# Layer 1's left-over modulation parts move from the recurrence to the mixers, and the mixers' PSUM banks are cut anew

## The chip, the cores and the metric

The kernel runs on one core of a Trainium2 chip. The metric is the time of one execution in microseconds of device time. Before the change three runs took 2719.62, 2722.55 and 2728.21 us, so the median is 2722.55. One execution was also profiled.

## The reference: what is computed

The reference is a two-layer backbone on 512 latent and 256 context tokens, 1024 channels wide, all in float32. Each layer has three token mixers beside each other (a bidirectional RWKV-7 recurrence, a latent attention, a Fourier mixing), merged through sigmoid gates, and then a gated feed-forward part with a convolution:

```
mod_lat = silu(c) @ w_ada[l] + b_ada[l]            # six vectors of 1024: shift, scale, gate, twice
h       = rms(x) * g_norm1 * (1 + sc1) + sh1
a, b, f, gate = split(h @ w_in)
m  = sig(gA)*(rwkv(a) @ w_a) + sig(gB)*(attention(b) @ w_b) + sig(gC)*(fourier(f) @ w_c)
x  = x + gt1 * (m @ w_out)
x  = x + gt2 * conv_ffn(rms(x) * g_norm2 * (1 + sc2) + sh2)
```

The last layer needs outputs for the latent tokens alone. The change is about when layer 1's modulation vectors (the first line) are computed. The first four of the 24 half-vectors are computed at the start, the other twenty in the background of the two layers.

## The kernel before

A float32 product of the large projections is made of three products of split operands (high by high, high by low, low by high; H and L in the names). The program is written in Python; a scheduler then sets the order in which each engine's instructions stand, so the order on TensorE (PE), VectorE (DVE), ScalarE (ACT), GpSimd (POOL) and SyncE (SP) is fixed before the program runs. Every engine works through its own list in order; SyncE's list issues most DMAs.

A layer goes through these stages: the projections of the recurrence (rwkv_project), the recurrence itself (rwkv_scan, twelve steps, each of a chain of small products in the PSUM tags f, i0, i1 and st), the mixers (fourier, rwkv_out, mla), and then the branches, w_out and the feed-forward part. PSUM has eight banks, and CUTS says how each stage divides them into tags; a tag with two buffers can be filled by one product while the product before it is still read.

Beside the recurrence the class Background issues work from a list. Its items are gate parts (L688, tag w: 24 products of 128x512 in layer 1, then ScalarE writes the tile gt and stores it) and modulation parts (ada_part). A modulation part loads 2 MB of w_ada in four loads of 512 KB into the buffers wr (three buffers, which gate weights and later the mixers' weights use too), makes eight products with them (L258), copies the row with ScalarE (L261), transposes it with four products (L265), and adds it up on VectorE (L268). In the recurrence the modulation parts run aside, in a tag of their own (a), with each load issued one ahead; layer 1 has eight of them (ADAS[1]). A gate part gives way to a step of a modulation part at its end, and with MID also once in its middle (L691). After each block of the recurrence's products, after() lets the background run for a fixed amount. When the recurrence has been written, drain() issues what is left: before the change all gate parts and, in layer 1, all modulation parts. What is left of them after a drain is made into items by mix(); those run in the mixers wherever fill() stands, in tag w, without a load ahead. In layer 0 two parts do.

The buffers hH and hL hold the layer's normalized input, which the gate parts read. They are given back (hst.close()) once no item needs them, and the mixers' tiles, gT among them, take their place. In layer 1 the mixers begin with kr, the rotary part of the keys (raw is loaded from m_dram, L460, and transposed by L464); then the key and query projections (L394, 72 products of 128x384 and 72 of 128x288), whose heads are transposed by L452; fourier (L639 to L660, tag r) stores its result by L669; rwkv_out loads the recurrence's outputs y (L1226, L1227), adds them (L1230), and takes three tiles of columns through tag r: L1233 (means), L801 (sums of squares), VectorE's reciprocal root and ScalarE's rex (L806), L813 (back to rows), read by L1238. Then comes the attention: scores by L567, transposes by L584, values by L595, again in tag r; four buffers pt hold the transposed probabilities.

Of the kernel before, what the change touches and what calls it, by code (L numbers as in the profile page):

```python
# [47 lines left out]
for _n, _w in CCOLS:  # L48
# [15 lines left out]
TAGF, TAGO = ("r", "r"), ("s", "r")  # L64
ROF = True
MFILL, AFILL = 2.5, 0.3
FIRST = ((12, 2.0), (8, 3.0))
MORE = False
XB, UB = 2, 2
MID = (True, True)  # L70
FILL = (1.0, 0.8)
PRE = (12.0, 24.0)
CUTS = dict(
    dense=(("mm", 2), ("s", 3), ("w", 1)),
    scan=(("f", 2), ("i0", 1), ("i1", 1), ("st", 2), ("w", 1), ("a", 1)),
    mixers0=(("mm", 2), ("s", 2), ("r", 1), ("w", 1)),
    mixers1=(("mm", 2), ("s", 2), ("r", 2)),
)
SCHED = dict(schedule_with_timeline_sim=True)

# [2 lines left out]
def hybrid_backbone_kernel(ctx: ExitStack, tc: tile.TileContext, A, out, dbg=None):  # L83
# [11 lines left out]
    def psum_phase(l, name):  # L95

        if banks:
            banks.pop("es").close()
            banks.clear()
        banks["es"] = ExitStack()  # L100
        for tag, bufs in CUTS[name]:
            banks[tag] = banks["es"].enter_context(tc.tile_pool(name=f"ps_{name}{l}_{tag}", bufs=bufs, space=bass.MemoryType.PSUM, reuse_waits="tile"))
# [175 lines left out]
    def near(es, l, name, bufs=1):  # L278
        return pool_on(es, name, l % 2, bufs)

    def far(es, l, name, bufs=1):
        return pool_on(es, name, 1 - l % 2, bufs)

    class Norm:
# [75 lines left out]
        def after_gain(self, parts, ks):  # L360
            for a, b in parts:
                s = 0 if a < LAT else 1
                for k in ks:
# [3 lines left out]
                    self.low(k, a, b)  # L367

    def mla(l, last, others, load_y, fill):
        q_tiles = range(4) if last else range(6)  # L370
        with ExitStack() as e1, ExitStack() as e2:
# [109 lines left out]
            def kv_rows(cH, cL, yc, WH, WL):  # L481
                hs = work.tile([128, 6, 6], F32, name="hs")
                for t in range(6):
                    ps = psmm()
                    proj(ps, t, cH, cL, WH, WL, 2, 0, 384, 0)
                    proj(ps, t, cH, cL, WH, WL, 2, 384, 768, 512)
                    jk = work.tile([128, 576], F32, tag="f", name="jk", bufs=2)[:, 0:384]
                    S.activation(out=jk, in_=ps[:, 0:384], func=AF.Square, scale=yc[:, t:t + 1])
                    V.tensor_reduce(out=hs[:, t], in_=jk.rearrange("p (h d) -> p h d", d=64), op=ALU.add, axis=AX.X)
                    S.activation(out=kn[:, t], in_=ps[:, 0:384], func=AF.Copy, scale=yc[:, t:t + 1])  # L490
                    S.activation(out=Vn[:, t], in_=ps[:, 512:896], func=AF.Copy, scale=yc[:, t:t + 1])
                    fill()
                V.tensor_tensor(out=hs, in0=hs, in1=ks.to_broadcast([128, 6, 6]), op=ALU.add)
                return hs.rearrange("p t h -> p (t h)")

            def q_rows(cH, cL, yc, WH, WL):
                qn = work.tile([128, nqn], F32, tag="qn" if FRONT[l] else "kn", name="qn").rearrange("p (t h d) -> p t h d", t=nq, d=QK)
                hs = work.tile([128, 6, 6], F32, name="hq")[:, 0:nq]
                for t in q_tiles:
                    ps = psmm()  # L500
                    proj(ps, t, cH, cL, WH, WL, 3, 0, 288, 0)
                    proj(ps, t, cH, cL, WH, WL, 3, 288, 576, 512)
                    jq = work.tile([128, 576], F32, tag="f", name="jq", bufs=2)
                    pv = ps.rearrange("p (a c) -> p a c", a=2)[:, :, 0:288]
                    S.activation(out=jq.rearrange("p (a c) -> p a c", a=2), in_=pv, func=AF.Square, scale=yc[:, t:t + 1])
                    V.tensor_reduce(out=hs[:, t], in_=jq.rearrange("p (h d) -> p h d", d=QK), op=ALU.add, axis=AX.X)
                    S.activation(out=qn[:, t].rearrange("p (a h) d -> p a (h d)", a=2), in_=pv, func=AF.Copy, scale=yc[:, t:t + 1])
                    fill()
                return qn, hs.rearrange("p t h -> p (t h)")
# [161 lines left out]
    def gate_part(l, it, W, hH, hL, streams, pool):  # L671
# [3 lines left out]
        for a, b in streams:  # L675
# [8 lines left out]
            else:  # L684
                WH, WL = W
                for n, (w, X) in enumerate(((WH, hH), (WL, hH), (WH, hL))):
                    for k in range(8):
                        TE.matmul(ps, lhsT=w[:, k, :], rhs=X[k][:, a:b], start=(k == 0 and n == 0), stop=(k == 7 and n == 2))  # L688
                        if (n, k) != (2, 7):
                            yield (b - a) / 2400  # L690
                        if MID[l] and (n, k) == (1, 3):  # L691
                            yield 0.0
# [6 lines left out]
    class Background:  # L699
# [81 lines left out]
        def after(self, ins):  # L781
            self.slots += 1
            with tc.high_priority(), tc.issue_after(ins.ins):
                self.run(FIRST[self.l][1] if self.slots <= FIRST[self.l][0] else FILL[self.l])

        def drain(self, items=0):

            while len(self.items) > items or (self.side and not items and (self.ada or self.adas)):
                self.run(1.0)
            while self.gen is not None:  # L790
                if next(self.gen, None) is None:
                    self.gen = None
            self.due = 0.0
# [489 lines left out]
    for l in range(DEPTH):  # L1283
        last = l == DEPTH - 1
# [7 lines left out]
        with ExitStack():  # L1292
            gp = far(yst, l, f"gt{l}")

            items = [("m", i) for i in (5, 6, 7, 2, 3, 4, 0, 1)] + [("g", x, c) for c in range(8) for x in range(3)]
            bg = Background(l, items, ADAS[l], hH, hL, streams, gp)
            with ExitStack() as e2:
                rwkv_project(l, last, W2, hH, hL, near(e2, l, f"rp{l}"))
                bg.take(NP[l], near(e2, l, f"rg{l}"))
            psum_phase(l, "scan")  # L1300
            bg.side = True
            bg.run(PRE[l])
            with ExitStack() as e2:
                rwkv_scan(l, last, near(e2, l, f"rs{l}"), lambda ins: bg.after(ins))
                bg.drain(LEFT[l])
                bg.mix()
            if not bg.items:
                hst.close()
            psum_phase(l, f"mixers{l}")

            def load_y():

                yp = far(yst, l, f"y{l}")
                yX = [[[yp.tile([128, T], F32R, name=f"y{x}{q}{i}") for i in range(kt)] for q in range(2)] for x, kt in enumerate((3, 3, 2))]
                for x, src in ((2, yc_dram), (0, ya_dram)):
                    for q in range(2):
                        for i in range(len(yX[x][q])):
                            P.dma_start(out=yX[x][q][i][:, ar], in_=src[q, i][:, ar])
                return yX

            def fill(us=MFILL):
                bg.run(us)

            side = far if last else near

            def others():
                with ExitStack() as e2:
                    if ROF and not last:
                        rwkv_out(l, last, side(e2, l, f"ro{l}"), fill)
                    fourier(l, last, side(e2, l, f"ft{l}"), yc_dram, fill)  # L1330
                    if last:
                        e2.close()
                    if last or not ROF:
                        rwkv_out(l, last, side(e2, l, f"ro{l}"), fill)

            if not last:
                others()
            yX = mla(l, last, others if last else None, load_y, fill)
            bg.drain()
            psum_phase(l + 1, "dense")  # L1340
            if not last:
                hst.close()
            if f"yB{l}" in dbg:
                for k in range(3):
                    nc.sync.dma_start(out=dbg[f"yB{l}"][k][:, ar], in_=yX[1][0][k][:, ar].bitcast(F32))
# [188 lines left out]
```

## Time and profile before

| what | us |
|---|---|
| median of three runs | 2722.55 |
| the profiled execution's own time | 2723.43 |
| its span, first to last instruction | 2721.6 |
| TensorE busy | 2581.3 |
| VectorE busy | 1467.6 |
| ScalarE busy | 1075.3 |
| GpSimd busy | 234.5 |

The profile is of one execution. "Busy" is the time in which an engine worked on an instruction; a matmul of float32 leaves more than one record, so the counts in its rows are above the counts in the program's order. In a row of the order of time, what stands in brackets at the end is how long the engine had been idle before, and what it was released by. Rows with SPq are issues of DMAs on SyncE. "PEclk" is the share of full clock that TensorE was granted.

### The profile page before, as it was taken

What the parts mean: (1) busy time and instruction counts of PE and PEld (TensorE: products, weight loads), DVE (VectorE), ACT (ScalarE), POOL (GpSimd) and SP (SyncE); (2) the same over time, 40 slices, a digit from 0 to 9 for tenths busy, and PEclk for the clock granted to TensorE, in tenths of its full rate; (3) what the DMA queues carried; (4) which work ended last, traced back from release to release, by engine and by line L of the source; (5) the groups of instructions that cost most, each with busy time, mean ns of one, the idle gap of its engine ahead of it and who ended that gap; (6) DMA issues with size and microseconds to landing.
All of it is one profiled execution on the core that took longest, in us unless ns stands there. A gap on an engine that the chain in (4) does not pass through costs nothing.

```text
span 2721.6 us, 56800 instructions
## 1 busy us (share of the span) xinstructions
PE 2581.3 (95%) x24016; PEld 2062.2 (76%) x24016; DVE 1467.6 (54%) x2965; ACT 1075.3 (40%) x1914; POOL 234.5 (9%) x316
## 2 busy tenths in 40 slices
PE   6999999997999989999999999999988899899999
PEld 3876777776877878888888877677666678778778
DVE  5443555434556665444444564446554767645546
ACT  4452343433464343222222445444433664423333
POOL 0122122200010000000000001312220010000000
PEclk9998999998999999999999999999999999999999
DMA  6366455365323532222212244764434326332334
GB/s 260 95 163 196 151 156 163 106 209 166 98 99 101 158 93 60 64 62 60 66 54 70 79 155 114 234 201 144 141 111 154 117 83 207 101 93 84 100 96 124
DMA packets 161267, 339.45 MB, mean 125 GB/s; under 512 B 32083, under 2 KB 76757, under 8 KB 161013
## 3 DMA queue, kind: packets, MB, share of 16 engines
q1 hardware_dynamic: 124852, 273.93, 32.4%
q0 software_dynamic: 10944, 36.58, 5.1%
q10 hardware_dynamic: 25216, 25.30, 2.8%
q8 instruction: 190, 3.11, 0.5%
q14 instruction: 65, 0.52, 0.1%
HBM read 273.88 MB, written 61.87 MB: 123 GB/s over the span
## 4 chain that ended last, share of the span: by engine, by line
PE 86%; DVE 5%; DMA 4%; ACT 3%; issue 2%; SPq 0%; ACTq 0%; DVEq 0%; POOL 0%; POOLq 0%
PE mm L220 47%; PE w L688 15%; PE st L957 3%; PE i L957 3%; PE mm L567 2%; PE a L258 2%; PE r L595 2%; PE mm L394 2%; PE s L584 1%; DMA wr<-in_w_ada 1%; PE s L871 1%; PE f L957 1%; PE i L954 1%; DVE wl L184 1%; PE f L954 1%
## 5 line engine op out<-in xcount | busy, mean ns | idle before, releaser
L183 ACT ACTIVATE wh<-wr 128x1024 fp32r<-128x1024 f32 (+4 forms) x334 | 302.0, 906 | 378.5 <-PE mm L220 282.8
L184 DVE TENSOR_TENSOR wl<-wr,wh 128x1024 fp32r<-128x1024 f32 (+3 forms) x332 | 342.6, 1034 | 89.2 <-ACT wh L183 86.8
L220 PE MATMUL mm<-fH,wh 128*128 128x512 f32 (+1 forms) x1072 | 225.0, 358 | 10.5 <-DVE ab L232 7.4
L231 DVE SCALAR_TENSOR_TENSOR ab<-mm,prm,ab 128x511 f32<-128x511 f32 (+1 forms) x132 | 86.8, 657 | 264.2 <-ACT ab L229 264.2
L220 PE MATMUL mm<-fH,wl 128*128 128x512 f32 (+1 forms) x1072 | 220.5, 353 | 0.0
L220 PE MATMUL mm<-fL,wh 128*128 128x512 f32 (+1 forms) x1072 | 219.3, 352 | 0.0
L220 PEld LDWEIGHTS mm<-fH,wh 128*128 128x128 f32 x1072 | 178.7, 192 | 42.1 <-issue 6.4
L220 PEld LDWEIGHTS mm<-fH,wl 128*128 128x128 f32 x1072 | 176.1, 189 | 29.9
L220 PEld LDWEIGHTS mm<-fL,wh 128*128 128x128 f32 x1072 | 175.0, 188 | 29.4
L688 PE MATMUL w<-hH,wh 128*128 128x512 f32 (+1 forms) x760 | 183.9, 377 | 10.2 <-ACT gt L693 9.7
L220 PE MATMUL mm<-gH,wh 128*128 128x512 f32 (+1 forms) x568 | 174.5, 346 | 10.0 <-ACT wh L183 4.8
L688 PE MATMUL w<-hL,wh 128*128 128x512 f32 (+1 forms) x760 | 180.5, 366 | 0.0
L688 PE MATMUL w<-hH,wl 128*128 128x512 f32 (+1 forms) x760 | 177.1, 366 | 0.0
L220 PE MATMUL mm<-gH,wl 128*128 128x512 f32 (+1 forms) x568 | 175.4, 348 | 1.1 <-DVE wl L184 0.9
L1252 DVE SCALAR_TENSOR_TENSOR x<-mm,mod,x 128x256 f32<-128x256 f32 (+1 forms) x136 | 80.0, 606 | 175.1 <-PE mm L220 174.4
L220 PE MATMUL mm<-gL,wh 128*128 128x512 f32 (+1 forms) x568 | 171.6, 343 | 0.0
L688 PEld LDWEIGHTS w<-hH,wh 128*128 128x128 f32 x760 | 125.3, 192 | 45.2 <-ACT gt L693 15.7
L229 ACT ACTIVATE ab<-mm,prm 128x768 f32<-128x768 f32 (+1 forms) x88 | 70.0, 795 | 219.9 <-PE mm L220 219.9
L688 PEld LDWEIGHTS w<-hH,wl 128*128 128x128 f32 x760 | 127.1, 191 | 23.5 <-issue 2.5
L688 PEld LDWEIGHTS w<-hL,wh 128*128 128x128 f32 x760 | 124.5, 189 | 24.0 <-issue 4.0
L220 PEld LDWEIGHTS mm<-gH,wh 128*128 128x128 f32 x568 | 97.3, 188 | 29.8 <-ACT wh L183 10.4
L220 PEld LDWEIGHTS mm<-gH,wl 128*128 128x128 f32 x568 | 97.3, 188 | 17.5 <-DVE wl L184 3.7
(388 smaller groups left out, 4631.4 us busy)
## 6 DMA issues: line engine op xcount, KB each, us to landing
wr<-in_w_up SPq DMA_DIRECT2D x88, 512.0 KB, 3.5
wr<-in_w_ada SPq DMA_DIRECT2D x80, 512.0 KB, 5.2
wr<-in_w_g SPq DMA_DIRECT2D x48, 512.0 KB, 4.1
wr<-in_w_out SPq DMA_DIRECT2D x32, 512.0 KB, 3.6
wr<-in_w_dn SPq DMA_DIRECT2D x48, 320.0 KB, 3.0
X<-rwx SPq DMA_DIRECT2D x48, 288.0 KB, 4.7
wr<-in_w_rw SPq DMA_DIRECT2D x24, 512.0 KB, 4.2
wr<-in_w_dn SPq DMA_DIRECT2D x32, 384.0 KB, 3.2
```

The costliest lines, as they stand in the source:

```text
L183: S.activation(out=H, in_=raw, func=AF.Copy)
L184: e.tensor_tensor(out=L, in0=raw, in1=H.bitcast(F32), op=ALU.subtract)
L220: TE.matmul(ps[:, a:b], lhsT=W[:, k, :], rhs=X[k][:, a:b], start=(k == 0 and n == 0), stop=(k == kt - 1 and n == 2))
L229: S.activation(out=o[:, a:b], in_=ps[:, a:b], func=AF.Identity, scale=w[1])
L231: V.scalar_tensor_tensor(out=o[:, a + 1:b], in0=ps[:, a:b - 1], scalar=w[0], in1=o[:, a + 1:b], op0=ALU.mult, op1=ALU.add)
L258: TE.matmul(ps[32 * i:32 * i + 32], lhsT=cs32[:, k, :], rhs=w[:, k - k0], start=(k < 4), stop=(k >= 4))
L394: TE.matmul(ps[:, o:o + hi - lo], lhsT=X(k)[:, t * 128:(t + 1) * 128], rhs=W[:, k, lo:hi], start=(k == 0 and n == 0), stop=(k == kt - 1 an ...
L567: TE.matmul(ps[:, a:b], lhsT=qT[:, h, t * 128:(t + 1) * 128], rhs=kT[:, h, a:b], start=True, stop=True)
L595: TE.matmul(po[64 * p:64 * p + 64, 0:128], lhsT=Vn[:, j, h * 64:(h + 1) * 64], rhs=pts[p][:, j * 128:(j + 1) * 128], start=(j == kts[0]), ...
L688: TE.matmul(ps, lhsT=w[:, k, :], rhs=X[k][:, a:b], start=(k == 0 and n == 0), stop=(k == 7 and n == 2))
L957: self.i = f(*a, **k)
L1252: V.scalar_tensor_tensor(out=x[:, a:b], in0=ps[:, a:b], scalar=mod[l][:, j, c, s:s + 1], in1=x[:, a:b], op0=ALU.mult, op1=ALU.add)
```

## The change

Four things change, all in layer 1. MID is off there, so that a gate part gives way to a modulation part once and not twice. drain() no longer issues the modulation parts that are left; mix() makes items of them, and they run in the mixers, at most 1.0 us of background (SPREAD) at each place of layer 1's mixers, where it was 2.5. These parts run in tag w, which layer 1's mixers did not have: it takes one of the two banks of tag r. And hH and hL are given back when only modulation parts are left.

```diff
+SPREAD = 1.0
-MID = (True, True)
+MID = (True, False)
 CUTS = dict(
-    mixers1=(("mm", 2), ("s", 2), ("r", 2)),
+    mixers1=(("mm", 2), ("s", 2), ("r", 1), ("w", 1)),
 )
         def drain(self, items=0):
-            while len(self.items) > items or (self.side and not items and (self.ada or self.adas)):
+            while len(self.items) > items:
                 self.run(1.0)
-            if not bg.items:
+            if all(it[0] == "a" for it in bg.items):
                 hst.close()
             def fill(us=MFILL):
-                bg.run(us)
+                bg.run(min(us, SPREAD) if last else us)
```

The first line moves all lines behind it by one: L258 of before is L259 of the change. In the order of the changed program six of the eight parts stand before L464, the sixth behind the last product of the recurrence, and two stand among the projections of keys and queries.

SyncE's issues at the end of layer 1's recurrence, before the change (w_ada is a modulation part's load, w_g a gate's weights, w_ukv and w_uq the mixers'):

```order
L191 DMA wr<-in_w_g 128x1024 x2
L245 DMA wr<-in_w_ada 128x1024 x4
L387 DMA wr<-in_w_ukv 128x768 x2
L387 DMA wr<-in_w_uq 128x576
L427 DMA gT<-in_gains 64x2x1
L460 DMA raw<-m_dram 128x768
L405 DMA raw<-m_dram 128x768
```

The same place in the changed program:

```order
L192 DMA wr<-in_w_g 128x1024
L246 DMA wr<-in_w_ada 128x1024 x4
L428 DMA gT<-in_gains 64x2x1
L246 DMA wr<-in_w_ada 128x1024 x5
L388 DMA wr<-in_w_ukv 128x768 x2
L461 DMA raw<-m_dram 128x768
L406 DMA raw<-m_dram 128x768
```

Five loads of modulation weights now stand between gT and raw, and those of w_ukv as well.

TensorE at the end of the Fourier products (tag r; L660 is the last of them), before the change:

```order
L394 MATMUL mm<-ml,cH 128x384
L657 MATMUL r<-dft,z 128x257
L658 MATMUL r<-alt,zh 128x257
L660 MATMUL r<-dft,z 128x255 x2
L657 MATMUL r<-dft,z 128x257 x2
L416 MATMUL s<-cst,sq 128x1 x4
L658 MATMUL r<-alt,zh 128x257
L660 MATMUL r<-dft,z 128x255 x2
L394 MATMUL mm<-mh,cH 128x384
```

And in the changed program, where the last of them stands:

```order
L395 MATMUL mm<-mh,cH 128x288
L395 MATMUL mm<-mh,cL 128x288
L395 MATMUL mm<-ml,cH 128x288
L266 MATMUL w<-cst,row 128x128 x4
L661 MATMUL r<-dft,z 128x255
L395 MATMUL mm<-mh,cH 128x288
```

Before, 24 of the key projection's 72 products and none of the query projection's stand ahead of the last Fourier product; now it is all 72 and 36 of the query's, and both modulation parts of the mixers.

TensorE at the third column tile of rwkv_out (L801, then L813), before the attention's first product with values (L595), before the change:

```order
L801 MATMUL r<-cst,y_23177 128x2 x4
L584 MATMUL s<-cst,pr 128x128 x12
L567 MATMUL mm<-kT,qT 128x512
L567 MATMUL mm<-kT,qT 128x256
L584 MATMUL s<-cst,pr 128x128 x6
L567 MATMUL mm<-kT,qT 128x512
L567 MATMUL mm<-kT,qT 128x256
L584 MATMUL s<-cst,pr 128x128 x6
L567 MATMUL mm<-kT,qT 128x512
L567 MATMUL mm<-kT,qT 128x256
L813 MATMUL r<-cst,rex 128x128 x4
L595 MATMUL r<-pt,Vn 64x128 x12
```

And in the changed program:

```order
L814 MATMUL r<-cst,rex 128x128 x4
L585 MATMUL s<-cst,pr 128x128 x6
L568 MATMUL mm<-kT,qT 128x512
L568 MATMUL mm<-kT,qT 128x256
L1234 MATMUL r<-y,cst 128x512
L568 MATMUL mm<-kT,qT 128x512
L568 MATMUL mm<-kT,qT 128x256
L802 MATMUL r<-cst,y_23180 128x2 x4
L814 MATMUL r<-cst,rex 128x128 x4
L596 MATMUL r<-pt,Vn 64x128 x12
```

The third L813 now stands right behind its L801, with the attention's products ahead of both; nine heads' scores and five groups of transposes stand before the first L595, where it was seven and four.

## Rows read from the trace of the kernel before

**Rows 1.** The page's first part: busy us, share of the span, instructions.
```profile
PE 2581.3 (95%) x24016; PEld 2062.2 (76%) x24016; DVE 1467.6 (54%) x2965; ACT 1075.3 (40%) x1914; POOL 234.5 (9%) x316
```

**Rows 2.** Busy time of each engine in five stretches of layer 1.
```profile
core 0: us, PE busy (x) PEld busy (x) DVE busy (x) ACT busy (x) POOL busy (x), PEclk, DMA share, GB/s
1720.00:2088.00 368.00, 352.17 (x6615) 255.24 (x6614) 190.13 (x438) 153.70 (x362) 85.91 (x116) 0.99 0.52 158
2088.00:2094.00 6.00, 0.52 (x2) 0.09 (x1) 2.50 (x3) 3.14 (x5) 0.10 (x1) 0.89 0.67 185
2094.00:2102.00 8.00, 6.66 (x23) 4.63 (x24) 6.78 (x17) 5.26 (x9) 0.00 (x0) 0.50 0.93 346
...
2133.00:2172.00 39.00, 28.81 (x153) 19.86 (x153) 33.63 (x118) 23.17 (x36) 1.60 (x3) 0.91 0.43 135
2172.00:2235.00 63.00, 62.89 (x484) 44.02 (x484) 38.99 (x102) 40.73 (x82) 5.51 (x10) 1.00 0.19 54
```

**Rows 3.** The recurrence's stretch again, the instructions of tile a alone (modulation parts).
```profile
1720.00:2088.00 368.00, 30.55 (x160) 7.46 (x160) 1.43 (x8) 4.78 (x8) 0.99 0.52 158
```

**Rows 4.** TensorE in order of time, end of the recurrence: start us, us, instructions.
```profile
2069.71 1.05 PE L258 MATMUL a<-wr,cs 128*32 128x512 f32 x4 [1.82 <-DMA wr<-in_w_ada]
...
2087.79 0.73 PE L688 MATMUL w<-hL,wh 128*128 128x512 f32 x2
2094.06 1.51 PE L464 MATMUL s<-cst,raw 128*128 128x128 f32 x6 [5.54 <-DMA raw<-m_dram]
```

**Rows 5.** SyncE's issues in order of time, 2085 to 2123 us.
```profile
2088.78 0.65 SPq L427 DMA_DIRECT2D gT<-in_gains  x1
2089.48 0.59 SPq L460 DMA_DIRECT2D raw<-m_dram  x1
...
2116.25 4.04 SPq L669 DMA_DIRECT2D yc_dram<-yC  x4
2120.39 0.38 SPq L1226 DMA_DIRECT2D y<-y_dram  x1
```

**Rows 6.** DMA issues, 2050 to 2070 us: count, size, median us to landing.
```profile
wr<-in_w_ada SPq DMA_DIRECT2D x4, 512.0 KB, 4.5
```

**Rows 7.** TensorE in order of time, layer 1's mixers.
```profile
2107.94 0.33 PE L394 MATMUL mm<-mh,cH 128*128 128x384 f32 x1
2108.12 0.33 PE L394 MATMUL mm<-mh,cL 128*128 128x384 f32 x1
...
2112.95 1.13 PE L660 MATMUL r<-dft,z 128*128 128x255 f32 x4
...
2127.47 1.02 PE L1233 MATMUL r<-y,cst 128*128 128x512 f32 x2
...
2132.83 0.29 PE L394 MATMUL mm<-mh,cL 128*128 128x288 f32 x1
2132.96 0.29 PE L394 MATMUL mm<-ml,cH 128*128 128x288 f32 x1
...
2146.18 1.11 PE L813 MATMUL r<-cst,rex 128*128 128x128 f32 x4 [4.98 <-ACT rex L806]
```

**Rows 8.** TensorE in order of time, where the attention's values begin.
```profile
2169.47 0.82 PE L584 MATMUL s<-cst,pr 128*128 128x128 f32 x6
...
2171.68 0.60 PE L813 MATMUL r<-cst,rex 128*128 128x128 f32 x4
2172.21 1.53 PE L595 MATMUL r<-pt,Vn 128*64 128x128 f32 x24
...
2174.39 1.46 PE L567 MATMUL mm<-kT,qT 96*128 96x512 f32 x4
```

**Rows 9.** VectorE in order of time: the first addition of y.
```profile
2125.54 0.69 DVE L1230 TENSOR_TENSOR y<-y,y 128x512 f32<-128x512 f32 x1 [1.25 <-DMA y<-y_dram]
```

**Rows 10.** Layer 0's mixers: TensorE's longest wait (us, times, longest), and one stretch.
```profile
PE w L258 <- DMA wr<-in_w_ada: 10.7, 4, 5.4
...
630.00:650.00 20.00, 12.53 (x42) 8.23 (x43) 9.01 (x29) 3.94 (x5) 0.00 (x0) 0.53 0.81 266
```

## The prediction, made before the changed kernel ran

> **What bounds the kernel now.** I read the page's first part, then the stretches of layer 1, then the order of time on TensorE and on SyncE around the two ends of the stretch that the change touches. TensorE is busy for 95% of the span [rows 1], so the first question is where it is not. In layer 1 the reader is to see three regimes [rows 2]. In the recurrence, 1720 to 2088 us, TensorE works 352.17 of 368 us: there it is the bound, and every product taken out should come back almost whole. Between 2088 and 2094 it does next to nothing, and from 2094 to 2102 its granted clock is 0.50, the lower of its two levels (1.2 of 2.4 GHz). From 2133 to 2172 it works 28.81 of 39 us; in the attention, 2172 to 2235, 62.89 of 63 us. So the mixers before the attention hold nearly all the free time: 5.5 us before 2094, 1.3 in 2094 to 2102, 10.2 in 2133 to 2172, some 17 us.
>
> What ends these gaps matters more than their size. The first ends with the arrival of the rotary-key rows: the last gate products start at 2087.79 and the first mixer product (L464) at 2094.06, after 5.54 us of waiting for raw [rows 4]. That load was issued at 2089.48, right behind the gT load at 2088.78 [rows 5]: SyncE is one queue in order, and gT lies where hH lay, so it waits for the last gate product. The gap inside 2133 to 2172 is the wait of 4.98 us before the first L813, the second half of rwkv_out's normalization [rows 7]. rwkv_out goes through bank r in three column tiles, each by L1233, L801 and L813, and attention's own r product (L595) comes only behind the third: L1233 starts at 2127.47 [rows 7], the third L813 at 2171.68, the first L595 at 2172.21 [rows 8]. From the first L1233 to the first L595 that is 44.7 us. And rwkv_out starts when its y rows are loaded: issued at 2120.39, behind the four stores of the Fourier result at 2116.25 [rows 5], added on VectorE at 2125.54 after a wait for that very DMA [rows 9].
>
> **The change part by part.** (1) The recurrence holds eight modulation parts: 30.55 us of TensorE in 160 records [rows 3], 3.82 us each. By the new order six stand ahead of L464 and two in the mixers. With MID off a part advances at half as many places, so the gates end earlier in the order and the fifth and sixth part stand around the last step; the last whole part follows the last recurrence product. Ahead of that product three parts fewer run: 3 x 3.82 = 11.5 us saved, since TensorE is the bound there.
>
> (2) The price stands on SyncE. Behind gT the new order has five modulation loads, then the w_ukv loads, and only then raw. They share three wr buffers, and a buffer is free only when TensorE has used it; a load lands 4.5 us after its issue [rows 6] and its products take 1.05 us [rows 4]. After the last recurrence product come the uses of the last part's first three loads (3 x 1.05), three issues of about 0.4 (0.38 in [rows 5]) and the 4.6 us from raw's issue at 2089.48 to L464 at 2094.06 [rows 4, 5]: 8.9 us, against 2094.06 - 2088.52 = 5.5 now. That is 3.4 us more. One wait for a load inside the last step, for which 1.82 us is the nearest row [rows 4], is added. Together L464 comes at -11.5 + 3.4 + 1.8 = -6.3, say 6 us earlier. At best, with no new wait, it is the two missing parts, 7.6; at worst, with a wait at each of the four last loads, about 2.
>
> (3) The two parts in the mixers put 7.6 us of products among the projections, and r loses a bank to w. With one r bank each Fourier tile waits until the one before it is read, and the new order has the Fourier products far back: now the last L660 stands behind 24 of the 72 products of 128x384 and none of 128x288; in the new order behind all 72 and 36 of 128x288. These run every 0.18 and 0.13 us [rows 7], so 48 x 0.175 + 36 x 0.133 = 13.2 us, and with the two parts 20.8 us, now stand in front of the last Fourier product. It ends now at 2114.1 [rows 7], 20.0 us after L464's start; then it would be 40.8.
>
> (4) From there to the load of y is 6.3 us now (2114.1 to 2120.39), with four stores in 4.04 us; then two of them, 2 us less: 4.3. The y load goes out 45.1 us after L464 instead of 26.3, so 18.8 us later counted from L464, and 18.8 - 6 = 12.8 later in absolute time. Of VectorE's queue the y addition holds back the later key heads and the query heads, which stand behind it, so attention's start is tied to it too.
>
> (5) From the load of y to the first L595 I keep what stands now, 7.1 us to L1233 and 44.7 to L595. The bounds of this unknown: less, because the first triple takes 18.7 us from L1233 to L813 with other work of VectorE in it, and the other two together 25.5 (2146.18 to 2171.68), 12.8 each [rows 7, 8]; were the first as short, 6 us less; more, because with one bank each triple also waits until L1238 has read the one before, and in the new order nothing stands between the third L801 and its L813, where the wait of 4.98 [rows 7] is the nearest row: 5 us longer. I take the stretch as it is now, since it lies between them and is the one that the rows show.
>
> (6) What TensorE can do before the first L595 is limited by the four pt buffers, but the new order puts two score products of a head (1.46 us) and one group of transposes (0.82) more ahead of it [rows 8]: 2 x 1.46 + 0.82 = 3.7 us given back, since from 2172 on TensorE is the bound. What stands behind the attention is the same work in nearly the same order; I cost it at nothing, hidden by the branch products that TensorE works on there.
>
> The sum: +12.8 - 3.7 = +9.1 us on the profiled execution's 2723.43 (span 2721.6), so 2732.5. The median of the runs shown is 0.9 lower, 2722.55; against it I forecast 2731.
>
> One rule speaks against step 3 and 5. By the row, bank r is waited for by three stages in turn [rows 7, 8]. The Trainium skill, TensorE: Matmul & The Clock Gate, section "HAM oscillation — how this bites in real kernels", reports of one kernel that adding PSUM double-buffering gave no further gain. By that, taking the second bank away would cost nothing either and the result would be the first rival's; no run here has shown it yet.
>
> **The rivals.** First, not slower: the gaps take the parts. The 17 us of free time before the attention take in the two parts, bank r's loss stays in the shadow of the projections, and the shorter recurrence comes through: -6 to -7.6, and up to another 3.3 if no gap brings the clock down (6.66 us of products ran at half clock in 2094 to 2102 [rows 2]). 2712 to 2720. For it: the gap before 2094 is there and TensorE has work ready. Against it: the gap's length is set by loads, and the new loads stand ahead of raw in the same queue. It decides from the point where the y load goes out less than about 10 us later than now.
>
> Second, a wash: rwkv_out's triples close up, as VectorE's other work inside the first triple moves ahead of it while it waits for y. The 6 us of step 5 are then saved, and the time is 2720 to 2727.
>
> Third, much slower: the parts in the mixers are not loaded ahead, and TensorE waits for each. Layer 0 does that now: its w products wait 10.7 us in four places, and from 630 to 650 us the clock granted is 0.53 for 12.53 us of products [rows 10]. With 10.7 us on top of the forecast: 2742 or more. Against it: in the new order a dozen or more projection products stand between most of these loads' uses.
>
> The Trainium skill, Trainium Kernel Development and Optimization, section "Best Practices", asks for double buffers so that DMA overlaps compute, which these parts do without; the row of layer 0 agrees, and by that rule this rival would be the likeliest.
>
> That the change doesn't do what it says: it does it for two of eight parts, no more; the other six still run in or right behind the recurrence.
>
> **How the numbers follow.** Forecast case (2727 to 2740, middle 2731): 0.44. First rival: 0.26. Wash: 0.17. Third: 0.13. About what a measurement of this kernel can tell from no change is 0.3%, 8.2 us: faster means under 2714.4, slower over 2730.7. Of the first rival half lies under 2714.4: faster 0.13. Of the forecast case two thirds lie above 2730.7, and all of the third rival: 0.29 + 0.13 = 0.42. Same: 0.45. The range: at the low end the two parts' 7.6 with most of the clock's 3.3, 2713; at the high end L464 only 2 us earlier (+4), the triples 5 us longer and part of the third rival, 2743.
>
> **What would show it.** Right: L464 some 6 us earlier, with TensorE waiting for w_ada loads just ahead of it; the y load of rwkv_out late, issued at about 2133 and the first L595 at about 2185; idle time before L813 or L801; attention as dense as now. Wrong: the first L595 at or before 2172 (first rival); waits of several us before the w products of L258 (third); a recurrence that isn't shorter ahead of its last step, because its own chain and not TensorE held it, would take away step 1.

## The result: slower by half a per cent, with a late y load

Five executions of the changed kernel have a median of 2737.78 us (2734.09 to 2741.51), five of the kernel before 2720.45 us (2718.54 to 2728.21): ratio 1.0051, 95% interval 1.003 to 1.0072. By this ratio the change costs 13.9 us (the two medians lie 17.3 us apart), where 8.5 were forecast. The profiled execution spans 2732.7 us against 2721.6. Code lines behind line 66 count one more than before.

The two executions differ by 3.3 us before layer 1's first gate product, where both run the same instructions: 1588.84 after, 1592.12 before. Counted from there the span's end is 14.4 us later (1143.9 against 1129.5). All stretches below are counted inside layer 1.

TensorE's order, after (start us, us, instructions, in brackets the wait and what ended it): end of the recurrence, last Fourier product, start of the attention's values.

```profile
1588.84 2.00 PE L689 MATMUL w<-hH,wh 128*128 128x512 f32 x8
...
2073.98 0.33 PE L958 MATMUL st<-MY,UV 128*64 128x64 f32 x3
...
2077.90 1.05 PE L259 MATMUL a<-wr,cs 128*32 128x512 f32 x4 [1.64 <-DMA wr<-in_w_ada]
2081.62 1.26 PE L259 MATMUL a<-wr,cs 128*32 128x512 f32 x4 [2.67 <-DMA wr<-in_w_ada]
...
2084.66 1.54 PE L465 MATMUL s<-cst,raw 128*128 128x128 f32 x6
...
2131.09 0.60 PE L661 MATMUL r<-dft,z 128*128 128x255 f32 x2
...
2182.16 1.12 PE L814 MATMUL r<-cst,rex 128*128 128x128 f32 x4 [3.35 <-ACT rex L807]
2184.20 2.83 PE L596 MATMUL r<-pt,Vn 128*64 128x128 f32 x24 [0.92 <-DVE y L1239]
2187.55 1.15 PE L585 MATMUL s<-cst,pr 128*128 128x128 f32 x6 [0.51 <-DVE pt L589]
2189.86 1.53 PE L596 MATMUL r<-pt,Vn 128*64 128x128 f32 x24 [1.16 <-DVE y L600]
```

The first mixer product is 9.4 us earlier than in [rows 4], 6.1 of it inside layer 1. The last Fourier product ends 17.6 us later than in [rows 7] (2131.69 against 2114.08), and the first L596 12.0 later than the L595 of [rows 8]. SyncE's issues, after:

```profile
2067.57 9.04 SPq L246 DMA_DIRECT2D wr<-in_w_ada  x5
2076.71 2.61 SPq L388 DMA_DIRECT2D wr<-in_w_ukv  x2
2079.37 0.42 SPq L461 DMA_DIRECT2D raw<-m_dram  x1
...
2134.09 1.05 SPq L670 DMA_DIRECT2D yc_dram<-yC  x2
2135.20 0.44 SPq L1227 DMA_DIRECT2D y<-y_dram  x1
...
2187.07 0.32 SPq L1245 DMA_DIRECT2D ya_dram<-yA  x1
```

The y load goes out at 2135.20 instead of 2120.39 [rows 5]. The last line is rwkv_out's last store. An eviction is the copy of a result out of PSUM. ScalarE's first eviction of the attention's values waits for that very store, and not for TensorE (ScalarE's order, after):

```profile
2189.20 0.28 ACT L599 ACTIVATE y<-r 128x128 fp32r<-128x128 f32 x1 [1.54 <-DMA ya_dram<-yA]
```

In the kernel before, the same store (SyncE) and the first eviction (ScalarE) are

```profile
2177.52 0.53 SPq L1244 DMA_DIRECT2D ya_dram<-yA  x1
2179.95 0.45 ACT L598 ACTIVATE y<-r 128x128 fp32r<-128x128 f32 x2 [0.54 <-issue]
```

The eviction starts 2.4 us behind the store there and 2.1 us behind it after. From the store to the span's end are 544.1 us before and 545.6 after. What has to be explained is thus when rwkv_out ends. Busy time by stretch, after (us, busy time of PE, PEld, DVE, ACT, POOL, granted clock, DMA share, GB/s):

```profile
2084.66:2096.66 12.00, 9.14 (x35) 6.85 (x34) 11.29 (x25) 7.64 (x13) 0.00 (x0) 0.50 0.88 289
2096.66:2108.66 12.00, 12.00 (x54) 7.73 (x54) 5.91 (x22) 6.54 (x12) 0.00 (x0) 0.74 0.64 193
...
2136.00:2184.20 48.20, 33.34 (x172) 22.76 (x170) 40.17 (x130) 25.62 (x41) 1.59 (x3) 0.90 0.44 140
2184.20:2246.25 62.05, 60.27 (x458) 42.82 (x458) 34.79 (x91) 38.45 (x76) 5.50 (x10) 0.97 0.19 55
```

and the first two stretches behind L464 in the kernel before:

```profile
2094.06:2106.06 12.00, 10.72 (x51) 8.62 (x52) 10.06 (x26) 7.91 (x14) 0.00 (x0) 0.63 0.77 278
2106.06:2118.06 12.00, 12.00 (x65) 10.60 (x64) 7.84 (x28) 8.63 (x19) 0.00 (x0) 1.00 0.21 66
```

The free time ahead of the attention has not been filled: 14.9 us are idle between 2136 and 2184, and after L465 the clock stays at its lower level (0.50) longer than before.

### The profile page after: what moved, and what is told of

Its sections match the earlier page's. It is cut to its first block, busy times and chain, and to the rows that moved or that the text cites. A ratio compares the mean times of both kernels' runs of the same rounds, so it can differ in the third digit from the quotient of the medians.

```text
span 2732.7 us, 56816 instructions
## 1 busy us (share of the span) xinstructions
PE 2587.8 (95%) x24016; PEld 2064.6 (76%) x24016; DVE 1466.4 (54%) x2965; ACT 1075.4 (39%) x1914; POOL 233.1 (9%) x316
## 4 chain that ended last, share of the span: by engine, by line
PE 85%; DVE 5%; DMA 4%; ACT 3%; issue 2%; SPq 0%; ACTq 0%; DVEq 0%
PE mm L221 47%; PE w L689 15%; PE i L958 2%; PE st L958 2%; PE mm L568 2%; PE mm L395 2%; PE a L259 2%; PE r L596 2%; PE s L585 1%; DMA wr<-in_w_ada 1%; PE s L872 1%; PE f L958 1%; DVE wl L185 1%; PE i L955 1%; PE f L955 1%
## 5 line engine op out<-in xcount | busy, mean ns | idle before, releaser
L221 PE MATMUL mm<-fH,wh 128*128 128x512 f32 (+1 forms) x1072 | 225.2, 359 | 10.3 <-DVE ab L233 7.2
L221 PEld LDWEIGHTS mm<-gH,wh 128*128 128x128 f32 x568 | 97.1, 188 | 29.4 <-ACT wh L184 10.4
```

What stands on the lines that cost most here:

```text
L221: TE.matmul(ps[:, a:b], lhsT=W[:, k, :], rhs=X[k][:, a:b], start=(k == 0 and n == 0), stop=(k == kt - 1 and n == 2))
```

## The experiments

Times of each profiled execution in us: G the first gate product of layer 1, R the row of the last recurrence products, K the first L464 or L465, Y the first y load, S rwkv_out's last store, E the span's end. The ratio is to executions of the kernel before on the same chip.

| run | ratio, 95% interval | G | R | K | Y | S | E |
|---|---|---|---|---|---|---|---|
| before | | 1592.12 | 2087.53 | 2094.06 | 2120.39 | 2177.52 | 2721.6 |
| changed | 1.0051, 1.003 to 1.0072 | 1588.84 | 2073.98 | 2084.66 | 2135.20 | 2187.07 | 2732.7 |
| e1 | 1.0058, 1.0044 to 1.0072 | 1592.13 | 2088.23 | 2094.65 | 2133.33 | 2193.90 | 2743.4 |
| e2 | 1.0008, 0.9996 to 1.0019 | 1590.01 | 2076.14 | 2087.62 | 2120.64 | 2181.57 | 2724.2 |
| e3 | 1.0034, 1.0021 to 1.0046 | 1590.70 | 2079.59 | 2091.22 | 2129.18 | 2185.56 | 2733.9 |
| e4 | 1.0066, 1.0053 to 1.0079 | 1588.21 | 2074.82 | 2087.78 | 2124.90 | 2190.24 | 2735.4 |
| e5 | 1.0049, 1.0035 to 1.0064 | 1586.56 | 2073.81 | 2085.19 | 2136.23 | 2190.08 | 2732.5 |
| e6 | 1.0002, 0.9991 to 1.0013 | 1579.59 | 2069.50 | 2080.41 | 2109.77 | 2179.15 | 2723.4 |
| e7 | 1.0027, 1.0015 to 1.0039 | 1584.62 | 2071.16 | 2075.28 | 2105.47 | 2182.70 | 2728.8 |
| e8 | 0.9983, 0.997 to 0.9996 | 1586.26 | 2065.68 | 2068.18 | 2102.11 | 2171.26 | 2716.0 |
| e9 | 1.0112, 1.0094 to 1.0129 | 1591.96 | 2079.10 | 2090.94 | 2123.64 | 2186.32 | 2757.2 |
| e10 | 1.0002, 0.999 to 1.0014 | 1592.37 | 2076.77 | 2081.98 | 2115.70 | 2182.84 | 2726.3 |
| e11 | 0.9985, 0.9974 to 0.9996 | 1582.11 | 2084.88 | 2091.37 | 2117.07 | 2174.24 | 2719.5 |
| e12 | 0.9976, 0.9963 to 0.9989 | 1585.25 | 2074.12 | 2078.98 | 2116.81 | 2176.51 | 2719.8 |

From S to E lie 542.4 to 549.5 us in all of them but e9 (570.9). The scheduler sets the order of every program anew, so one edit can move more than it names. Times of one per cent and less are read from the ratios; the milestones tell where.

**e1, the bank alone.** Kernel before, with

```
-    mixers1=(("mm", 2), ("s", 2), ("r", 2)),
+    mixers1=(("mm", 2), ("s", 2), ("r", 1), ("w", 1)),
```

> The kernel before with one edit alone: in layer 1's mixers bank r goes from two to one and the freed bank w is given to nothing. No modulation part moves. Theory A (the forecast's: the loss of r's second bank is the cost, because Fourier tiles then wait for one another and rwkv_out's y rows are loaded late): L464 stays at about 2094; the new order has the last L660 behind all 72 products of 128x384 instead of 24, 48 x 0.175 = 8.4 us more; the y load 6 to 8 us later than 2120.4, the first L595 5 to 8 us later than 2172.2, the whole 5 to 8 us slower (about 1.002 to 1.003 of before). Theory B (the cost is the parts themselves, their loads ahead of raw and the half clock that follows; the bank is innocent): within 2 us of before.

It costs 0.58%, 15.8 us: as much as the whole change, with no part moved. Theory A is right in kind, and its 5 to 8 us were too few. (The profiled execution is the longest of e1's six: 2745.30 us, their median 2741.13.) SyncE's issues in e1 (the four stores of the Fourier result stretch over 7.77 us, against 4.04 in [rows 5], as each waits for its tile):

```profile
2125.46 7.77 SPq L669 DMA_DIRECT2D yc_dram<-yC  x4
2133.33 0.39 SPq L1226 DMA_DIRECT2D y<-y_dram  x1
...
2193.90 0.32 SPq L1244 DMA_DIRECT2D ya_dram<-yA  x1
```

The last L660 stands 34.4 us behind L464 instead of 18.9: 15.5 more, where 8.4 of products had been counted. Most of the rest shows in the first 24 us behind L464 (stretches of e1), with the clock at 0.50 and 0.78 and 3.8 us idle, against 0.63, 1.00 and 1.3 idle in before:

```profile
2094.65:2106.65 12.00, 10.25 (x39) 7.91 (x39) 9.41 (x21) 7.17 (x13) 0.00 (x0) 0.50 0.78 276
2106.65:2118.65 12.00, 9.99 (x48) 9.72 (x48) 7.66 (x32) 6.99 (x14) 0.00 (x0) 0.78 0.16 45
```

Busy time multiplied by the clock makes 12.92 us of full-speed work in these 24 us, against 18.75 in before: 5.8 of the 7.1 us that are still missing. Waits for the one bank are hardly among them. The two longest waits of TensorE there that before does not have are

```profile
2101.66 0.80 PE L646 MATMUL r<-cst,fE 128*128 128x128 f32 x2 [0.47 <-ACT zh L640]
2113.59 1.05 PE L416 MATMUL s<-cst,sq 128*128 128x1 f32 x8 [1.76 <-DVE sq L412]
```

The first, 0.47 us, is for ScalarE's reading of a Fourier tile; the longer is for VectorE's squares. So what the bank costs here lies in the order that the scheduler makes without it, and in the slower start.

**e2, the bank given back.** Changed kernel, with

```
-    mixers1=(("mm", 2), ("s", 2), ("r", 1), ("w", 1)),
+    mixers1=(("mm", 2), ("s", 2), ("r", 2)),
-                return ada_part(it[1], it[2], it[3], "w")
+                return ada_part(it[1], it[2], it[3], "s" if self.l else "w")
```

> The changed kernel with one edit: bank r keeps its two banks as before, and the two left-over modulation parts use bank s in the mixers, so that no bank is given up. Their work and the shorter recurrence stay. Theory A: L464 as in the changed kernel (about 2085), y load about 2112 to 2116, first L595 about 2164 to 2168 and the whole 5 to 10 us faster than before, 2710 to 2716. Theory B: the parts' 7.6 us and their loads cost the same as in the changed kernel, first L595 at 2180 or later, the whole 2728 to 2738.

Level with before: the loss is gone, as A says, but the gain that A expected isn't there. Against the changed kernel, from which e2 differs in the bank and in the tag of the parts alone, that is 11.7 us (13.9 less 2.2), where the bank by itself cost 15.8 in e1. The last L661 is back at 19.2 us behind L465; y is still loaded 13.8 us behind it (7.4 in before), since a modulation load stood ahead of it (SyncE, e2; in e6, with that load on another queue, y goes out 29.4 us behind L465 instead of 33.0):

```profile
2115.28 1.18 SPq L670 DMA_DIRECT2D yc_dram<-yC  x2
2120.26 0.33 SPq L246 DMA_DIRECT2D wr<-in_w_ada  x1
2120.64 0.54 SPq L1227 DMA_DIRECT2D y<-y_dram  x1
```

**e3, the parts out.** Changed kernel, which leaves out the last two parts and sets their rows to zero; mix() with

```
+            if self.l:
+                for a in self.items:
+                    V.memset(mod[1][:, a[2], 4 * a[3]:4 * a[3] + 4], 0.0)
+                self.items = []
```

> The changed kernel with the two left-over modulation parts (the last two of layer 1) left out, their rows set to zero; r keeps its one bank. 7.6 us of TensorE work and eight loads of 512 KB are missing. Theory A (bank r's loss alone sets the y load): L464 about 2085, the last L661 behind all 72 products of 128x384 but before those of 128x288, y load about 2118 to 2120, first L596 about 2170 to 2174, the whole 2718 to 2724, level with before although work is missing. Theory B (the parts): first L596 about 2163, the whole 2709 to 2713.

9.3 us slower than before with 7.6 us less work: B is out. A's place for the last L661 was right (33.7 us behind L465, 34.4 in e1), its time was missed as in e1. Put together, as an estimate: bank +15.8 (e1), bank and shorter recurrence +9.3 (e3), so the recurrence brings about -6.5; the parts add 4.6 to e3 and give the change's 13.9. The split is rough: each of these times is known to 3.4 to 5.7 us, and in e3's trace L465 came only 1.4 us earlier from G than in before (500.5 against 501.9).

**e4, MID alone.** Kernel before with `MID = (True, False)`.

> The kernel before with MID off in layer 1 alone: all eight parts are still issued before the mixers and r keeps two banks, but a part advances at half as many places, so that by the new order four parts stand around or behind the last recurrence product. Theory A: the recurrence's last product some 13 us earlier, about 2074, as in the changed kernel; three parts behind it, each 3.82 us of TensorE plus waits for loads, so L464 within 4 us of 2094 and the Fourier products some 5 us behind where they were; the whole 2722 to 2732. Theory B (the waits for modulation loads and the half clock after them are the cost): 2732 or more, as in the changed kernel, since four parts wait for their loads there.

18.0 us slower, in total as B said. The recurrence's last product is as early as in the changed kernel, as A said; L464 came at 2087.78, earlier than A's 2094. But the parts behind it wait for their loads on either side of L464 (TensorE, e4), with the clock at 0.52 from 2081.00 to 2087.70 and at 0.59 from 2093.80 to 2100.00, and the first Fourier product (L639) stands behind them:

```profile
2081.88 1.92 PE L258 MATMUL a<-wr,cs 128*32 128x512 f32 x4 [2.27 <-DMA wr<-in_w_ada]
...
2087.78 1.00 PE L464 MATMUL s<-cst,raw 128*128 128x128 f32 x6
2090.38 1.05 PE L258 MATMUL a<-wr,cs 128*32 128x512 f32 x4 [1.59 <-DMA wr<-in_w_ada]
2093.82 1.05 PE L258 MATMUL a<-wr,cs 128*32 128x512 f32 x4 [2.39 <-DMA wr<-in_w_ada]
...
2106.50 0.60 PE L639 MATMUL r<-cst,fT 128*1 128x128 f32 x4
```

So MID off, taken alone, costs as much as the whole change. These costs don't add: with the last two parts left to the mixers and both banks of r kept (e2), 2.2 of the 18.0 us remain. The changed kernel with MID on was not run.

**e5, attention out of r's queue.** Changed kernel with `TAGO = ("s", "w")`: rwkv_out's tiles in bank w.

> The changed kernel with one edit: rwkv_out's tiles (L1234, L802, L814) use bank w instead of bank r, so that attention's own r product (L596) no longer comes behind the third triple in r's order; by the new order it stands ahead of the second triple's L814. Theory A (attention starts when rwkv_out's chain through r is done, and that chain starts with the late y load): y load unchanged near 2135, first L596 near 2166 instead of 2184; five score heads fewer stand ahead of it (some 11 us of products that then lie in the attention), so only the idle time ahead of it comes back: 5 to 9 us faster than the changed kernel, 2727 to 2732. Theory B (what stands ahead of the attention is TensorE's and VectorE's work on the key and query heads, and the chain through r is beside it): within 2 us of the changed kernel, 2735 to 2740.

No gain, as B said, yet not for B's reason. The first L596 came at 2166.59, and the next waited until 2192.86 (TensorE, e5):

```profile
2185.77 0.66 PE L814 MATMUL w<-cst,rex 128*128 128x128 f32 x4 [0.66 <-ACT rex L807]
2192.86 2.83 PE L596 MATMUL r<-pt,Vn 128*64 128x128 f32 x24 [6.44 <-DVE y L600]
```

since the first eviction waited for rwkv_out's last store (ScalarE, e5):

```profile
2192.21 0.28 ACT L599 ACTIVATE y<-r 128x128 fp32r<-128x128 f32 x1 [2.88 <-DMA ya_dram<-yA]
```

So rwkv_out's end binds the attention twice, through bank r and through the evictions, which wait for its stores. The code's pool order suggests that they share places in SBUF; that was not tried.

**e6, e7, e8: queue and number of parts.** e6 is e2 with the mixers' modulation loads on GpSimd's queue; e7 lets the recurrence take in no more than five parts; e8 is e7 with MID on. The edit of the loads also took in the parts of layer 1 that layer 0's mixers run, which was not meant. They are two parts with eight loads, not the four that the text of e11 below names.

```
-            nc.sync.dma_start(out=w, in_=A["w_ada"]...
+            (P if l and tag != "a" else nc.sync).dma_start(out=w, in_=A["w_ada"]...
-            while self.ada or self.adas:
+            while self.ada or len(self.adas) > (0, 3)[self.l]:          (e7, e8)
```

> The kernel of e2 (r with two banks, the left-over parts in bank s) with one more edit: their eight loads are issued on GpSimd's queue instead of SyncE's. In e2 the last L661 came 19.2 us after L465, as in the kernel before (18.9), and still y was loaded 13.8 us behind it instead of 7.4: a modulation load stood ahead of it on SyncE, waiting for a buffer. Theory A (that queue is what held y): y load about 2115 instead of 2120.6, first L596 about 2170, the whole 4 to 6 us faster than e2, 2717 to 2721 against 2720 to 2724 of before. Theory B (the parts' products on TensorE are the cost): as e2.

> The kernel of e6, and three parts instead of two are left to the mixers: none runs between the recurrence's last product and L465. In the changed kernel 10.4 us lie between these two, in before 6.3. Theory A: L465 some 4 us earlier than in e6 (about 2081 to 2083), y load and first L596 earlier by about as much, the whole 2712 to 2718. Theory B (each part costs its 3.82 us wherever it stands): as e6.

> The kernel of e7 with MID on as in before: five parts run inside the recurrence, spread as before, and three in the mixers. Theory A (MID only shifts which parts run late in the recurrence): three parts of 3.82 us fewer in a recurrence bound by TensorE, the last recurrence product near 2087.5 - 11.5 = 2076, L465 near 2082, the whole as e7 within 3 us, 2712 to 2718. Theory C (the recurrence is bound by its own chain between 1900 and 2008, where TensorE is busy for 91 to 94%, and fewer parts there save nothing): last product at 2082 or later, 4 to 6 us slower than e7.

In total e6 is as e2, as B said; e7 is slower than both theories had it; e8 is 12.0 us faster than e7, where A said within 3 and C slower.

All three load y early, e8 33 us ahead of the changed kernel. Counted from G the load goes out at 530.2 (e6), 520.9 (e7) and 515.9 us (e8), against 528.3 in before, 530.6 in e2 and 546.4 in the changed kernel, so e6's is early through layer 0 alone. An early y does not pay: from Y to S they take 69.4, 77.2 and 69.2 us, against 57.1 in before and 51.9 in the changed kernel. Counted from G, e6 ends as the changed kernel, e7 too, and e8 as before; what their totals gained lies ahead of G.

So theory A's chain is not enough. Part of what stretches rwkv_out is VectorE's list. The first triple takes 26.1 us in e8 (L1234 at 2111.40, L814 at 2137.45) and 14.8 in the changed kernel. In it the steps of the reciprocal root, from L804 to the last L180, stand among the heads' work and take 17.6 us against 8.5 (VectorE, two lines of e8, then two of the changed kernel):

```profile
2119.19 0.17 DVE L804 TENSOR_SCALAR hv<-r 128x8 f32<-128x8 f32 x1 [2.77 <-PE r L802]
2136.58 0.16 DVE L180 SCALAR_TENSOR_TENSOR rsy<-rst,rsy 128x8 f32<-128x8 f32 x1
...
2145.25 0.17 DVE L804 TENSOR_SCALAR hv<-r 128x8 f32<-128x8 f32 x1 [0.41 <-PE r L802]
2153.61 0.17 DVE L180 SCALAR_TENSOR_TENSOR rsy<-rst,rsy 128x8 f32<-128x8 f32 x1
```

What stretches the rest stays open. e8 against theory C: two or three parts fewer made the recurrence 11.0 (e10), 6.5 (e12) and 16.0 us (e8) shorter from G to R; C is out.

**e9, the bank taken from s.** Changed kernel with `("s", 1), ("r", 2), ("w", 1)`.

> The changed kernel with one edit: the bank w of layer 1's mixers is taken from s (two to one) and r keeps its two. The parts have a bank of their own as in the change. Theory A (it is r's second bank that the time hangs on, because the Fourier products, and behind them rwkv_out, go through r): the last L661 about 20 us behind L465 as in e2, the whole as e2, 2721 to 2728. Theory B (the mixers and the attention need every bank that they had; s serves the attention's transposes): AV stretch longer than 62 us and the whole 2733 or more.

Worst of all, by 30.5 us: B. The mixers are near e2's (y load 32.7 us behind L465, 33.0 in e2); the attention's values take 84.8 us instead of 62.1 in the changed kernel (stretch and waits of e9; a wait's line gives us, times, longest):

```profile
2182.00:2266.84 84.84, 70.26 (x495) 47.54 (x494) 45.25 (x112) 46.17 (x89) 5.64 (x10) 1.00 0.14 40
```

```profile
PE s L585 <- ACT pt L587: 6.9, 10, 0.7
PE mm L568 <- ACT pr L573: 6.5, 9, 0.7
```

These two waits are 13.4 of the stretch's 14.6 idle us. TensorE's busy time is 10.0 us longer too (70.26 against 60.27), which the runs don't explain.

**e10, e11, e12.** e10 is e2 with MID on and the recurrence taking in six parts (`> (0, 2)[self.l]`); e11 is the kernel before with layer 0's mixers loading their parts on GpSimd's queue; e12 has both.

> r with two banks, the parts in bank s, all loads on SyncE (as e2), MID on as in before, and the recurrence takes in only six of the eight parts; the last two are left to the mixers, so that no part stands behind the recurrence's last product. Theory A: recurrence 2 x 3.8 = 7.6 us shorter than before, L465 7 us earlier; in the mixers y is loaded some 4 us later counted from L465 than in before (the wait of modulation loads on SyncE that e2 showed), first L596 3 to 5 us earlier; the whole 2716 to 2721 against 2723 of before. Theory B (the two parts cost their 7.6 us in the mixers again): as before, 2722 to 2725.

> The kernel before with one edit: in layer 0's mixers alone, the loads of the modulation parts are issued on GpSimd's queue instead of SyncE's. In e6 to e8 this was part of the edit, unintended, since four parts of layer 1 run in layer 0's mixers; their layer 1 began 3 to 10 us earlier than in the other runs (first gate product 1580 to 1586 us against 1587 to 1592). Theory A (SyncE's queue, on which a load waits for its buffer, holds layer 0's mixers too): 4 to 8 us faster than before, 2715 to 2719. Theory B (that spread is the scatter between runs): within 2 us of before. Layer 1 is not touched, beside what the scheduler moves.

> The edits of e10 and e11 together. Theory A: the gains add, 2709 to 2715 against 2723 of before, faster than before and than the changed kernel. Theory B: as the better of e10 and e11, 2716 or more.

e10 brings nothing, as B said: K is 12.3 us earlier from G (489.6 against 501.9), yet S is 5.3 us later than in before, much as in e7 (5.2). e11 is 4.1 us faster, as A said, from layer 0's mixers: the recurrence of layer 0 ends 0.9 us later than in before, the attention's first scores (L567) start 7.8 us earlier (752.9 against 760.7). TensorE's wait there falls from the 10.7 us of [rows 10] to (waits of e11)

```profile
PE w L258 <- DMA wr<-in_w_ada: 7.9, 2, 4.2
```

Layer 1 begins 10.0 us earlier in e11's profiled execution, and takes 7.4 us more from G to R (502.8 against 495.4); its order of gates and parts there is not quite before's. The total thus isn't the worth of the queue in layer 0 alone.

e12 is 6.5 us faster than before, and so faster than the changed kernel: the best of all. Its interval overlaps e11's; that layer 1's edit adds to it is not shown.

## Why the forecast was right, and where its sizes were off

The direction and the mechanism hold: a shorter recurrence, then a y load that is later by more. Term by term, from the two profiled executions:

1. The recurrence. Forecast -11.5 us to its last product; measured from G -10.3 (485.1 against 495.4).
2. SyncE ahead of L465. Forecast 3.4 + 1.8; from R to K 10.7 us against 6.5, so 4.2. Waits for w_ada loads stand just ahead of it, the longest 2.67. The 10.7 us came as forecast (8.9 + 1.8); the 5.5 set against them ran from the last gate product's end (2088.52), and from the last recurrence product it was 6.5. Together L465 is 6.1 us earlier in layer 1, where 6 was forecast: two errors of about 1 us cancel.
3. and 4. Bank r and the y load. Forecast 18.8 us later counted from L465; measured 24.2 (50.5 against 26.3). This is the term that was too small. The last L661 ended 47.0 us behind L465's start, not 40.8. I had counted the products that stand ahead of it, at full clock. In the 24 us behind L465 the clock was 0.50 and 0.74, with 2.9 us idle, against 0.63, 1.00 and 1.3 in before. Busy time multiplied by the clock makes 13.45 us of full-speed work instead of 18.75: 5.3 of the 6.2 us that are missing; the rest is open. e1 has the same slow start (0.50 and 0.78), but the bank is not its only cause: e7 (0.50 and 0.80) and e10 (0.50 and 0.76) have it with two banks.
5. From the y load to the first L596. Forecast 51.8 as before; measured 49.0. The first triple closed up by 3.9 us (14.8 instead of 18.7), inside the bounds.
6. The give-back of 3.7. It did not come: from the first to the last L596 62.05 us, against 62.24. The score products are indeed ahead, but behind the wait of 3.35 us before the third L814 the clock was 0.50 (2182.16 to 2187.03), the first 24 values took 2.83 us instead of 1.53, and the next waits are those for rwkv_out's store.

The sum: -6.1 + 24.2 - 2.8 - 0.2 = 15.1, and 0.7 less behind the last L596 gives the 14.4 measured; forecast -6 + 18.8 - 3.7 = 9.1. The profiled execution took 2734.49 us, where 2732.5 was forecast for it. That it came so near is partly luck: its layer 0 was 3.3 us short.

The rivals. The first (not slower) had its point at a y load about 10 us later than now; it was 14.8 later. The idle time it counted on was there, but not in reach: the parts ran between 2097 and 2130, where TensorE has projections to do, and the gap opened behind them. The wash was half seen (3.9 of 6 us in the first triple). The third rival had no part in it: no product of L259 in the mixers waits for a load.

The forecast weighed a rule that spoke against it, in the Trainium skill, TensorE: Matmul & The Clock Gate, section "HAM oscillation — how this bites in real kernels": in one kernel, PSUM double-buffering gave no further gain. Here e1 disagrees by 15.8 us for r, and e9, which also gives the parts a bank of their own, by 28.3 for s (30.5 less e2's 2.2).

## What to carry to other kernels

Before a PSUM bank is given away, look for the stage that ends last and runs through it. Here that stage's products moved behind the work that was ready, and the rows that come next (y) were loaded late. Price a bank by taking it away alone, with nothing else moved, as e1 does; and price the other parts of a change as well, since they need not add: here the bank alone cost 15.8 us, MID off alone 18.0, and the whole 13.9. Work moved into idle time must be ready where the gap is; idle time behind a late chain is not room ahead of it.

## What was not expected

- A modulation part taken out of the recurrence gave back more than its 3.82 us on TensorE: 11.0 us for two (e10) and 16.0 for three (e8), from G to R. But e12, with the same two out, gave back 6.5, and e11, with none out, took 7.4 more; so these figures hold the changed order of the gates too.
- Executions differ ahead of layer 1 more than in its recurrence: the first gate product of the nine kernels with the same layer 0 (before, changed, e1 to e5, e9, e10) came between 1586.6 and 1592.4 us; from G to R the six with the same places of gates and parts in the recurrence (changed, e2 to e5, e9) took 485.1 to 488.9.
- Loads issued on GpSimd's queue instead of SyncE's were worth 4.1 us (e11), with the same loads and products, in an order that the scheduler set anew.
